# Two more units of the MLP's down projection done plainly, between the fast up units and the fast passes

## The chip, the cores and the metric

The kernel runs on one core of one Trainium2 chip. The metric is the device time of one execution in microseconds: the median of three runs is 1788.47 us (1786.55 to 1789.25).

## The reference

Two requests, a prompt of 256 tokens and a sample of 512, pass through the same two-layer encoder. All is float32. Cut to what matters here:

```
for layer in range(2):
    x = x + attention(rmsnorm(x)) @ w_out         # layer 0: neighbourhood and grouped-query heads
                                                  # layer 1: differential heads
    h = rmsnorm(x, ln_mlp[layer])                 # 768 tokens x 1024 features
    x = x + square(relu(h @ w_up)) @ w_down       # w_up 1024x4096, w_down 4096x1024
return rmsnorm(x, ln_f)
```

The change touches only the MLP line, in both layers.

## The kernel before

**Layout.** Features lie on the 128 partitions, the 768 tokens of both requests side by side along the row. `x` is eight tiles of 128x768. A float32 product is made of three float32r products: each operand is split into a high part (ScalarE copies it to float32r) and a low part (VectorE subtracts), and TensorE adds high x high, high x low and low x high. So each weight tile costs a copy (lines 90, 95) and a subtraction (line 91), or, for some quarters, a second ScalarE copy and an accumulating DMA issued by GpSimd (`wsplit_acc`, lines 95 to 97).

**Fast products.** Most of the MLP is done by Strassen's scheme in Winograd's form: a 2x2 block product takes seven products instead of eight. A *unit* is 256 of the 4096 hidden features. `up_fast` (line 948) makes one unit: seven products of 12 matmuls (`product`, line 940; line 945 is the matmul), 128x384 each, with results in the PSUM tiles upx, upy and upz. It then prepares seven *forms* of the unit's activations, the operands that the down projection's seven products will want, in one staging tile `hf` (two buffers), and SyncE stores them to DRAM (line 998, 1344 KB). `quarters` (line 905) loads the weights of one unit or pass as two tiles `wraw` (three buffers) and builds four tile pairs `whi`/`wlo` (four buffers) of sums and differences of the weight quarters, on VectorE (line 921) and ScalarE.

`down_fast` (line 1038) makes one *pass*: for a pair of output tiles p (0 to 3) it takes the units k0 to k1 of the table `PASSES` (14 entries), runs seven products of 3 matmuls for each unit (PSUM tiles dnx, dny, dnz), and adds each product to `x` (`onto`, line 1046: VectorE). `Forms.need` (line 1017) loads the forms back (line 1020) into `hf`, and splits them on ScalarE (line 1032) and VectorE (line 1033) into the tiles that the string `HOMES` names in order: `h` the four pairs hh/hl, `T` the six pairs Th/Tl, `x` the eight pairs xh/xl. T and x hold the input of the up units until the last of them.

**Plain products.** Per layer, four hidden tiles (half the size of a unit each) at the start are done plainly: `up_plain` and `down` (line 1080; matmul in `proj_feat`, line 222; results dna, dnb; additions in line 1090). The last two units ("rest") go up by the fast scheme without forms and down plainly, in layer 0 with `down` again, in layer 1 in `final` (line 1094). So a layer runs: plain group up and down, 12 fast units up, 2 rest units up, 14 passes, last plain group. `mlp` (line 1145) holds this order.

**What sets the order.** Each engine executes its own queue in order. The order in the queues is made by a scheduler from the program's order, priorities and buffers that come free; all waits are semaphores. SyncE's queue carries all weight loads, form loads and form stores; GpSimd's the accumulating DMAs.

## Time and profile before

| | |
|---|---|
| median of three runs | 1788.47 us (1786.55 to 1789.25) |
| profiled execution | 1786.56 us |
| its span, first to last instruction | 1784.8 us |
| TensorE busy (PE) | 1733.3 us, 11098 matmuls |
| VectorE busy (DVE) | 1267.9 us |
| ScalarE busy (ACT) | 946.9 us |
| mean granted TensorE clock | 0.991 |

The stages of the span that matter here, by the first and last matmul of each name:

| stage | layer 0, us | layer 1, us |
|---|---|---|
| plain group, down | 413.9 to 447.0 | 1312.1 to 1345.2 |
| 14 fast up units (12 with forms, 2 rest) | 446.9 to 650.8 | 1345.2 to 1549.2 |
| 14 fast passes | 650.8 to 843.8 | 1549.2 to 1740.5 |
| last plain group | 843 to 875.5 | 1738 to 1775 (with the final norm) |

How to read it: a matmul's recorded duration (334 ns for 128x384) overlaps with the next one's, so a busy share says little; what counts is how many matmuls a stretch of time holds.

### The profile page before, as it was taken

The page shows a single profiled execution, that of the slowest core. Times are in us where ns is not written, and L with a number is a line of the kernel's source. Part 1 is how long each engine was busy: PE and PEld are TensorE (multiplying, and loading weights), DVE is VectorE, ACT ScalarE, POOL GpSimd, SP SyncE. Part 2 cuts the span into 40 slices and gives each one's busy share as a digit, 9 for nine tenths or more (in the row PEclk, how much of TensorE's full clock was granted, in tenths as well). Part 3 has the DMA queues.
Part 4 walks back from the last instruction along what each step waited for, and adds up shares of the span by engine and source line. Part 5 has one row for each costly group of instructions (what it writes and reads, how often), then busy time and mean ns, then how long its engine had stood idle before and what let it go on. Part 6 is the DMA issues. An engine that isn't in the chain of part 4 may idle for free.

```text
span 1784.8 us, 28991 instructions
## 1 busy us (share of the span) xinstructions
PE 1733.3 (97%) x11098; PEld 1645.2 (92%) x11098; DVE 1267.9 (71%) x2458; ACT 946.9 (53%) x1981; POOL 248.4 (14%) x330
## 2 busy tenths in 40 slices
PE   7999999999999989999999999999999999989998
PEld 7878888899999989999999999988899999989997
DVE  7877646479566668886566767676696666688875
ACT  6765544344566665453435555554455666655534
POOL 3421000020000001111221312220200000011111
PEclk9999999999999999999999999999999999999999
DMA  5111222312565676764411101112124666777542
GB/s 166 48 34 40 65 86 90 124 34 66 143 188 183 213 251 177 234 172 99 153 48 48 48 25 46 54 57 95 36 66 132 184 186 186 244 216 230 157 102 83
DMA packets 61546, 214.49 MB, mean 120 GB/s; under 512 B 7136, under 2 KB 12512, under 8 KB 55264
## 3 DMA queue, kind: packets, MB, share of 16 engines
q1 hardware_dynamic: 47296, 190.08, 32.1%
q0 software_dynamic: 12096, 19.93, 7.1%
q10 hardware_dynamic: 2016, 2.64, 0.5%
q8 instruction: 87, 1.43, 0.3%
q14 instruction: 51, 0.42, 0.1%
HBM read 169.37 MB, written 42.47 MB: 119 GB/s over the span
## 4 chain that ended last, share of the span: by engine, by line
PE 84%; DVE 6%; DMA 4%; ACT 2%; issue 2%; POOL 1%; POOLq 0%; SPq 0%; DVEq 0%; ACTq 0%
PE upx L945 13%; PE dnx L945 9%; PE dqk L209 8%; PE upz L945 6%; PE dnz L945 4%; PE dvp L209 4%; PE upc L880 4%; PE opa L222 4%; PE upy L945 3%; PE dna L222 3%; PE dnb L222 3%; PE npa L222 2%; PE dny L945 2%; PE ds L288 2%; PE dpv L731 2%
## 5 line engine op out<-in xcount | busy, mean ns | idle before, releaser
L91 DVE TENSOR_TENSOR wlo<-wraw,whi 128x1024 fp32r<-128x1024 f32 (+3 forms) x232 | 224.3, 967 | 140.0 <-ACT whi L90 139.6
L90 ACT ACTIVATE whi<-wraw 128x1024 fp32r<-128x1024 f32 (+3 forms) x228 | 193.6, 849 | 177.8 <-PE dnx L945 70.5
L209 PE MATMUL dqk<-whi,xh 128*128 128x256 f32 x384 | 115.6, 301 | 0.0
L209 PE MATMUL dqk<-whi,xl 128*128 128x256 f32 x384 | 108.6, 283 | 0.0
L209 PE MATMUL dqk<-wlo,xh 128*128 128x256 f32 x384 | 108.4, 282 | 0.0
L716 ACT ACTIVATE de<-ds,m 128x512 f32<-128x512 f32 (+1 forms) x96 | 58.3, 612 | 79.7 <-DVE m L714 79.6
L97 POOL DMA_DIRECT2D wlo<-in_w_down_dram x56 | 49.3, 913 | 364.3 <-ACT wlo L96 277.3
L95 ACT ACTIVATE whi<-wraw 128x512 fp32r<-128x512 f32 (+3 forms) x84 | 49.2, 586 | 91.4 <-PE upy L945 36.6
L97 POOL DMA_DIRECT2D wlo<-in_w_up_dram x28 | 24.7, 883 | 452.6 <-DVE hf L963 301.1
L1046 DVE TENSOR_TENSOR x<-x,dnx 128x384 f32<-128x384 f32 x112 | 61.6, 550 | 33.9 <-PE dnx L945 33.1
L209 PEld LDWEIGHTS dqk<-whi,xh 128*128 128x128 f32 x384 | 73.1, 190 | 8.5 <-issue 7.7
L945 PE MATMUL upx<-Th,whi 128*128 128x384 f32 x224 | 74.9, 335 | 0.0
L945 PE MATMUL upx<-Th,wlo 128*128 128x384 f32 x224 | 74.8, 334 | 0.0
L945 PE MATMUL upx<-Tl,whi 128*128 128x384 f32 x224 | 74.8, 334 | 0.0
L945 PE MATMUL upx<-xh,whi 128*128 128x384 f32 x224 | 74.8, 334 | 0.0
L945 PE MATMUL upx<-xl,whi 128*128 128x384 f32 x224 | 74.8, 334 | 0.0
L945 PE MATMUL upx<-xh,wlo 128*128 128x384 f32 x224 | 74.8, 334 | 0.0
L90 ACT ACTIVATE whi<-ws 128x1024 fp32r<-128x1024 f32 (+3 forms) x56 | 56.0, 999 | 35.3 <-PE dnz L945 17.1
L209 PEld LDWEIGHTS dqk<-wlo,xh 128*128 128x128 f32 x384 | 73.3, 191 | 0.0
L209 PEld LDWEIGHTS dqk<-whi,xl 128*128 128x128 f32 x384 | 73.1, 190 | 0.0
L921 DVE TENSOR_TENSOR ws<-wraw 128x1024 f32<-128x1024 f32 (+3 forms) x56 | 64.1, 1145 | 11.3 <-DMA wraw<-in_w_down_dram 7.9
L158 POOL TENSOR_TENSOR acc<-acc,sq 128x384 f32<-128x384 f32 (+2 forms) x28 | 39.0, 1394 | 233.4 <-ACT sq L153 232.6
(350 smaller groups left out, 6103.0 us busy)
## 6 DMA issues: line engine op xcount, KB each, us to landing
wraw<-in_w_up_dram SPq DMA_DIRECT2D x64, 512.0 KB, 3.6
h<-hf SPq DMA_DIRECT2D x24, 1344.0 KB, 5.1
hf<-h SPq DMA_DIRECT2D x24, 1344.0 KB, 7.6
wraw<-in_w_down_dram SPq DMA_DIRECT2D x56, 512.0 KB, 3.8
wraw<-in_w_in_o_dram SPq DMA_DIRECT2D x24, 512.0 KB, 3.7
wlo<-in_w_down_dram POOLq DMA_DIRECT2D x40, 256.0 KB, 5.0
wraw<-in_w_in_e_dram SPq DMA_DIRECT2D x16, 512.0 KB, 3.7
wlo<-in_w_up_dram POOLq DMA_DIRECT2D x28, 256.0 KB, 6.0
```

Source lines behind the costliest of these rows:

```text
L90: nc.scalar.activation(hi, raw, AF.Copy)
L91: nc.vector.tensor_tensor(out=lo, in0=raw, in1=hi.bitcast(F32), op=ALU.subtract)
L95: nc.scalar.activation(hi, raw, AF.Copy)
L97: nc.gpsimd.dma_start(lo, src, accum_op=ALU.add)
L158: eng.tensor_tensor(out=self.acc[:, s], in0=self.acc[:, s], in1=sq, op=ALU.add)
L209: nc.tensor.matmul(ps[:, :256], st[:, tk], col(k, part, 0, 256), start=(k == 0 and i == 0), stop=(k == KD - 1 and i == 2))
L222: nc.tensor.matmul(ps[:, : e - s], lhs(k, part), mv[:, s:e], start=(k == 0 and i == 0), stop=(k == nk - 1 and i == 2))
L716: nc.scalar.activation(e, s, AF.Exp, bias=m, scale=1.0, accum_out=l2[:, c : c + 1])
L880: last = nc.tensor.matmul(ps, lhs(f0 + f, k, part), mv[:, s:e], start=(n == 0 and j == 0), stop=(n == KD - 1 and j == 2))
L921: add = lambda out, u, v: nc.vector.tensor_tensor(out=out, in0=u, in1=v, op=ALU.add)
L945: nc.tensor.matmul(ps, w[part][:, c], mv, start=(start and kk == 0 and j == 0), stop=(stop and kk == len(form) - 1 and j == 2), skip_group ...
L1046: nc.vector.tensor_tensor(out=xm[:, c], in0=xm[:, c], in1=ps, op=op)
```

## The change

1. The rest units keep their place at the end (now called "far"), but two more units are taken out of the fast passes. These "near" units go up by the fast scheme last, just before the passes. Their activations are not stored: `hparts` splits them at once from the staging tile into hh/hl, and a plain `down` of them runs between the up units and the first pass. Ten units with forms remain, and 12 passes.
2. `HOMES` starts with T and x (hh/hl are in use by the near group).
3. `keep_in_program_order` pins the first matmul of each product, and of each plain group's tile, so that TensorE's queue follows the program's order there.
4. Passes of two or three units use no accumulating DMA; their quarters are all split by ScalarE and VectorE.
5. ScalarE issues the stores of forms, and of the far units.
6. `wraw` has four buffers; the far units use the staging tile.

```diff
-NU = FF // P // 2 - GF
+NU = FF // P // 2 - 6
...
 PASSES = ((0, 0, 2), (1, 0, 3), (2, 0, 4), (3, 0, 4), (0, 2, 6), (1, 3, 7), (2, 4, 8), (3, 4, 8),
-          (0, 6, 10), (1, 7, 11), (2, 8, 12), (3, 8, 12), (0, 10, 12), (1, 11, 12))
+          (0, 6, 10), (1, 7, 10), (2, 8, 10), (3, 8, 10))
 
-HOMES = "hhh" + "TTTTTTxxxxxxxx" + "hhhh" + "TTTTTTxxxxxxxx" + "TTTTTTx"
+HOMES = "TTTTTTxxxxxxxx" + "hhhh" + "TTTTTTxxxxxxxx" + "TTT"
...
-        raw = rpool.tile([P, 1024], F32, tag="wraw", name="wraw", bufs=3)[:, :width]
+        raw = rpool.tile([P, 1024], F32, tag="wraw", name="wraw", bufs=4)[:, :width]
...
-                        nc.tensor.matmul(ps[:, : e - s], lhs(k, part), mv[:, s:e],
-                                         start=(k == 0 and i == 0), stop=(k == nk - 1 and i == 2))
+                        mm = nc.tensor.matmul(ps[:, : e - s], lhs(k, part), mv[:, s:e],
+                                              start=(k == 0 and i == 0), stop=(k == nk - 1 and i == 2))
+                        if pin and k == 0 and i == 0:
+                            tc.keep_in_program_order(mm)
...
+                if kk == 0 and j == 0:
+                    tc.keep_in_program_order(mm)
...
+        hs = [htiles(mp) for _ in range(2)] if kind == "near" else []
+
+        def done(i):
+            if hs:
+                hparts(*hs[i], st[:, 2 * i : 2 * i + 2])
...
-        if forms:
-            nc.sync.dma_start(kept, st)
-        else:
-            for i, t in enumerate(f):
-                nc.sync.dma_start(kept[:, 2 * i : 2 * i + 2].rearrange("p a b -> p (a b)"), t)
-        return kept
+        nc.scalar.dma_start(kept, st[:, :n])
+        return [kept]
+
+    def hparts(hi, lo, f):
+        f = f.rearrange("p a b -> p (a b)")
+        nc.scalar.activation(hi, f, AF.Copy)
+        nc.vector.tensor_tensor(out=lo, in0=f, in1=hi.bitcast(F32), op=ALU.subtract)
...
-        forms = Forms([up_fast(xs, T, mp) for _ in range(NU)], mp)
-        rest = [up_fast(xs, T, mp, False) for _ in range(GF // 2)]
+        units = lambda n, kind: [t for _ in range(n) for t in up_fast(xs, T, mp, kind)]
+        forms = Forms(units(NU, "forms"), mp)
+        rest = units(GF // 2, "far")
+
+        down(units(GF // 2, "near"), x, True)
         for p, k0, k1 in PASSES:
             forms.need(k1)
-            down_fast(x, p, forms.f[k0:k1], mp)
-            if (p, k1) == (3, NU):
+            down_fast(x, p, forms.f[k0:k1], mp, (11, 12) if k1 - k0 > 3 else ())
+            if (p, k1) == (1, NU):
                 hs = last_group(rest, mp)
...
-        nxt, nn = [], Norm(lambda: mp.tile([P, NT], F32, tag="sq", name="sq", bufs=1))
+        nxt, nn = [], Norm(lambda: staging(mp)[:, 0:2].rearrange("p a b -> p (a b)"))
```

The order of the weights in `w_down` follows the new table. In the changed file the lines behind the edits have moved: the matmuls of `product` are line 949, those of the plain groups line 223, the splits of forms lines 1049 and 1050, `hparts` lines 1018 and 1019.

TensorE's queue at the end of the up units of layer 0, before (upx is the last up product, dnx and dny the first fast pass):

```order
L945 MATMUL upx<-xl,whi 128x384
L945 MATMUL upx<-xh,wlo 128x384
L945 MATMUL dnx<-hh,whi 128x384
L945 MATMUL dnx<-hl,whi 128x384
L945 MATMUL dnx<-hh,wlo 128x384
L945 MATMUL dnx<-Th,whi 128x384
```

and now (dna and dnb are the near group's plain products):

```order
L949 MATMUL upx<-xl,whi 128x384
L949 MATMUL upx<-xh,wlo 128x384
L223 MATMUL dna<-hh,whi 128x384
L223 MATMUL dnb<-hh,whi 128x384
L223 MATMUL dna<-hl,whi 128x384
L223 MATMUL dnb<-hl,whi 128x384
```

192 matmuls of the near group now stand between the two phases.

ScalarE's queue from the end of the last near unit on, in the change (hf_7017 is that unit's staging tile, hh_7018 and hh_7020 its split halves, hf_7372 the first unit's forms on their way back, whi_7250 to whi_7312 plain weights, whi_7411 the first pass's weights):

```order
L90 ACTIVATE whi_7250<-wraw_7248 128x1024
L974 ACTIVATE hf_7017<-hf_7017 128x384
L1049 ACTIVATE Th_7382<-hf_7372 128x768
L1018 ACTIVATE hh_7018<-hf_7017 128x768
L973 ACTIVATE hf_7017<-upx_7013 128x384
L90 ACTIVATE whi_7312<-wraw_7310 128x1024
L974 ACTIVATE hf_7017<-hf_7017 128x384
L1049 ACTIVATE Th_7386<-hf_7372 128x384
L1018 ACTIVATE hh_7020<-hf_7017 128x768
L90 ACTIVATE whi_7411<-wraw_7406 128x256
```

The near unit's last half stands behind weight splits and form splits that the before had elsewhere in its queue.

ScalarE's queue at a unit's start in the up stage, before (hf_6343 is the new unit's staging tile, whi_6453 the next unit's weights):

```order
L964 ACTIVATE hf_6343<-upx_6339 128x384
L95 ACTIVATE whi_6453<-wraw_6448 128x512
L96 ACTIVATE wlo_6454<-wraw_6448 128x512
L90 ACTIVATE whi_6453<-wraw_6450 128x512
L967 ACTIVATE hf_6343<-hf_6343 128x384
```

and now:

```order
L970 ACTIVATE hf_6343<-upx_6339 128x384
L95 ACTIVATE whi_6453<-wraw_6448 128x512
L96 ACTIVATE wlo_6454<-wraw_6448 128x512
L1013 DMA h7_6310<-hf_6207 128x2688
L973 ACTIVATE hf_6343<-hf_6343 128x384
L970 ACTIVATE b12_6344<-upx_6339 128x384
```

The store of the unit before (hf_6207) now stands in ScalarE's queue, behind the copies that feed the accumulating DMA, and one weight split has moved further back.

More of the change, by code (lines that the diff above doesn't have):

```diff
@@ L944, in product, with up_fast @@
             for j, (part, mv) in enumerate(((0, fh), (0, fl), (1, fh))):
-                nc.tensor.matmul(ps, w[part][:, c], mv, start=(start and kk == 0 and j == 0),
-                                 stop=(stop and kk == len(form) - 1 and j == 2), skip_group_check=True)
-    def up_fast(xs, T, mp, forms=True):
+                mm = nc.tensor.matmul(ps, w[part][:, c], mv, start=(start and kk == 0 and j == 0),
+                                      stop=(stop and kk == len(form) - 1 and j == 2), skip_group_check=True)
+                if kk == 0 and j == 0:
+                    tc.keep_in_program_order(mm)
+    def up_fast(xs, T, mp, kind="forms"):
         ws = quarters("w_up", 512, mp, (11,))
@@ L955, in up_fast @@
         s5 = mp.tile([P, NH], F32, tag="st", name="s5", bufs=3)
+        st = staging(mp)
+        forms = kind == "forms"
         if forms:
-            st = staging(mp)
             b11, b21, t2, t1, t3, b22, t4 = (st[:, i] for i in range(7))
@@ L960, in up_fast @@
         else:
-            f = [mp.tile([P, NT], F32, tag=t, name="f", bufs=GF) for t in ("hh", "hl")]
-            b11, b12, b21, b22 = (t[:, c] for t in f for c in (ta, tb))
+            b11, b12, b21, b22 = (st[:, i] for i in range(4))
         op = lambda out, u, v, o: nc.vector.tensor_tensor(out=out, in0=u, in1=v, op=o)
@@ L987, in up_fast @@
         nc.vector.scalar_tensor_tensor(out=b12, in0=b12, scalar=0.0, in1=b12, op0=ALU.max, op1=ALU.mult)
+        done(0)
         if forms:
@@ L992, in up_fast @@
         relu2(b21, X, -1.0)
+        done(1)
         if forms:
             less(t4, t2, b21)
-        kept = dram.tile([P, 7 if forms else 4, NH], F32, name=f"h{len(store)}")
+        if hs:
+            return hs
+        n = 7 if forms else 4
+        kept = dram.tile([P, n, NH], F32, name=f"h{len(store)}")
         store.append(kept)
-        if forms:
-            nc.sync.dma_start(kept, st)
-        else:
-            for i, t in enumerate(f):
-                nc.sync.dma_start(kept[:, 2 * i : 2 * i + 2].rearrange("p a b -> p (a b)"), t)
-        return kept
+        nc.scalar.dma_start(kept, st[:, :n])
[4 more added lines that the diff above has]
+        nc.vector.tensor_tensor(out=lo, in0=f, in1=hi.bitcast(F32), op=ALU.subtract)
     store = []
@@ L1277, in _layout @@
     for w in wd:
-        parts.append(plain(w[:GF]))
+        parts += [plain(w[:GF]), plain(w[-GF:])]
         for ps in PASSES:
```

16 lines of the change are left out of this document (7 added, 9 removed).

## The prediction

> **What bounds the kernel now.** I first read the stretches of the two MLPs with their counts, then what TensorE waited for in them, then the chain of waits at the worst place. The windows are: layer 0's plain group, its up units, the head of its passes, the rest of the passes; then layer 1's head and rest. Columns: bounds and length in us, busy time and count by engine, granted clock, DMA share, GB/s.
>
> ```profile
> span 1784.8 us, 28991 instructions
> 413.87:447.00 33.13, 33.13 (x193) 33.13 (x193) 31.42 (x53) 13.55 (x26) 1.08 (x1) 1.00 0.22 59
> 446.88:650.70 203.82, 203.82 (x1178) 203.82 (x1177) 135.14 (x194) 127.01 (x229) 13.12 (x15) 1.00 0.61 186
> 650.70:708.90 58.20, 48.91 (x252) 46.51 (x251) 43.81 (x67) 29.88 (x48) 7.02 (x8) 0.91 0.78 226
> 708.90:840.40 131.50, 130.90 (x752) 129.61 (x750) 102.94 (x155) 62.56 (x94) 15.83 (x18) 1.00 0.59 162
> 1549.10:1591.00 41.90, 32.31 (x167) 29.97 (x166) 31.52 (x49) 21.67 (x36) 5.26 (x6) 0.96 0.80 242
> 1591.00:1737.40 146.40, 145.56 (x836) 144.32 (x834) 115.18 (x173) 70.78 (x105) 17.61 (x20) 1.00 0.60 166
> ```
>
> The 14 up units are 14 x 84 = 1176 matmuls (the window also counts one at each edge); 203.82 / 1176 = 0.1733 us each, with TensorE never idle. That is the pace of a 384-column matmul. The plain group keeps it as well: 192 x 0.1733 = 33.3 us, though VectorE is busy for 31.42 of them. The heads of the passes do not. Layer 0: 252 x 0.1733 = 43.7 us of work in 58.2, so 14.5 us lost. Layer 1: 167 x 0.1733 = 28.9 in 41.9, 13.0 lost. The rest of the passes loses 131.5 - 130.3 = 1.2 and 146.4 - 144.9 = 1.5. So **27.5 us are lost in the two heads and 2.7 behind them**, and elsewhere in the MLPs there is nothing to win but matmuls.
>
> What TensorE waited for, layer 0's passes and then layer 1's (us in total, times, longest), then the clock after the waits in layer 0, then pieces of the chain of waits there (start, length):
>
> ```profile
> PE dnx L945 <- DMA wlo<-in_w_down_dram: 6.0, 2, 3.0
> PE dnx L945 <- ACT whi L90: 2.0, 1, 2.0
> PE dnx L945 <- DVE x L1046: 1.7, 3, 0.7
> ...
> PE dnx L945 <- DMA wlo<-in_w_down_dram: 4.9, 2, 3.2
> PE dny L945 <- DMA wlo<-in_w_down_dram: 2.5, 1, 2.5
> PE dnx L945 <- ACT whi L90: 2.1, 1, 2.1
> ...
> 665.00:670.00 5.00, 3.77 (x14) 3.26 (x14) 1.67 (x4) 1.27 (x2) 0.00 (x0) 0.69 0.89 318
> 670.00:675.00 5.00, 3.64 (x11) 3.37 (x12) 4.79 (x7) 4.53 (x8) 0.87 (x1) 0.50 0.26 97
> ...
> 646.95 7.36 DMA wlo<-in_w_down_dram
> 657.70 7.80 DMA wlo<-in_w_down_dram
> ```
>
> The accumulating DMAs of the first two passes' weights take 7.4 and 7.8 us from issue to landing, in a stretch where the DMA engines are busy at 0.78 with form loads, weights and the last stores; the passes there are short (two and three units, 42 and 63 matmuls, 7.3 and 10.9 us), so nothing covers them. After 3 us of waiting the granted clock falls to 0.69 and 0.50 for a while: 14 and 11 matmuls in 5 us instead of 29. The lost 14.5 us are these waits plus the slow matmuls behind them.
>
> **The change, term by term.**
>
> *Matmuls.* Two units leave the passes: 2 x 7 products x 3 matmuls x 4 pairs = 168. The near group needs 4 tiles x 8 outputs x 2 halves x 3 = 192. Per layer 24 more, 24 x 0.1733 = 4.2 us; both layers **+8.3 us**, certain, since nothing else is on TensorE. The up stage keeps its 14 units.
>
> *The head's losses.* The first pass now starts 33.3 us after the last up product, behind the near group. In that time must be ready: the forms of units 0 and 1 for pass 0 and of 2 and 3 soon after, and the weights of passes 0 and 1. Durations and sizes:
>
> ```profile
> hf<-h SPq DMA_DIRECT2D x24, 1344.0 KB, 7.6
> h<-hf SPq DMA_DIRECT2D x24, 1344.0 KB, 5.1
> wlo<-in_w_down_dram POOLq DMA_DIRECT2D x40, 256.0 KB, 5.0
> L1090 DVE TENSOR_TENSOR x<-dna,x 128x384 f32<-128x384 f32 x8 | 4.5, 557 | 4.8 <-PE dna L222 4.6
> L91 DVE TENSOR_TENSOR wlo<-wraw,whi 128x1024 fp32r<-128x1024 f32 x18 | 22.0, 1220 | 2.8 <-ACT whi L90 2.8
> L91 DVE TENSOR_TENSOR wlo<-wraw,whi 128x512 fp32r<-128x512 f32 x12 | 8.2, 687 | 0.0
> L1046 DVE TENSOR_TENSOR x<-x,dnx 128x384 f32<-128x384 f32 x56 | 30.8, 550 | 16.6 <-PE dnx L945 16.2
> L1033 DVE TENSOR_TENSOR xl<-hf,xh 128x768 fp32r<-128x768 f32 x15 | 14.3, 953 | 1.1 <-ACT xh L1032 1.1
> L1032 ACT ACTIVATE xh<-hf 128x768 fp32r<-128x768 f32 x15 | 12.1, 835 | 4.8 <-PE dnx L945 2.2 <-PE dny L945 2.1 <-PE dnz L945 0.5
> L90 ACT ACTIVATE whi<-wraw 128x1024 fp32r<-128x1024 f32 x18 | 19.1, 1061 | 31.5 <-PE dnx L945 18.5 <-DVE wraw L921 4.7 <-PE dnb L222 3.8
> L96 ACT ACTIVATE wlo<-wraw 128x512 fp32r<-128x512 f32 x20 | 12.3, 615 | 0.0
> L968 ACT ACTIVATE f<-f 128x384 f32<-128x384 f32 x1 | 0.5, 523 | 0.0
> ```
>
> Bytes: four forms of 1344 KB are 5.5 MB and the two passes' weights (four tiles, 2 x 256 and 2 x 384 KB) 1.3 MB; at the head's 226 GB/s that is 30 us. The near group's own four weight tiles and the first form load go earlier, during the last up unit. So the bytes fit in 33.3 us, and form 3 is wanted only 18 us later. VectorE's queue between the last up product and pass 0 holds, by the program's order: 16 additions (8.9 us at 0.557), two plain weight subtractions (2.4), 13 full and 4 half form subtractions (12.4 + 2.2, the half ones taken as 0.55 like an addition of that width), the near unit's two (1.9), pass 0's weights and the start of pass 1's (5.3, by their widths from the rows of 512 and 1024 columns): 33.1 us. That is full, but what stands last in it belongs to later passes, and the first plain group ran without a wait at 31.42 of 33.13. Passes 0 and 1 have no accumulating DMA any more. I take the heads' losses as gone: **-27.5 us**. Bounds: half of them stay (-13.8), or the later waits go as well (-30.2).
>
> *New waits.* (a) The near group reads its fourth activation tile early: matmul 30 needs its high half 5.2 us after the last up product, matmul 32 its low half at 5.5. ScalarE gets there late: from the end of the fifth product (4.2 us before the end) its queue holds three weight copies of about 1.0 us, four full copies of forms and near halves at about 0.8, and six shorter ones at about 0.5, together some 9.2 us, so the high half comes at 5.1 and the low half, 0.95 us of VectorE later, at 6.1: a wait of 0.6 us if the first form lands in time for its split, which stands ahead in the same queue. Its load starts when the first near unit's staging tile comes free, about 11 us before the end, and takes 5.1 to 7.6 us; the split is due 5.8 us before the end. So 0.6 to 2.5 us; I take 1.2 per layer. (b) Pass 2 is the first with accumulating DMAs. Its weight slot comes free 3.1 us into pass 1; two copies of 0.6 us, the issue, and 5.0 us to landing (7.8 at worst above) end at about 10 to 12.5, wanted at 11.3 us: 0 to 1.2 us, I take 0.4. Waits of this size carry no loss of clock: in layer 1 a stretch with 2.2 us of idling kept the full clock:
>
> ```profile
> 1565.00:1570.00 5.00, 2.83 (x15) 2.08 (x13) 4.09 (x7) 1.96 (x4) 0.00 (x0) 1.00 0.61 252
> ```
>
> Together 1.6 per layer, **+3.2 us**, bounds 1.2 to 7.4.
>
> *The tail.* Passes 10 and 11 are now of two units: 7.3 us of TensorE against some 8.0 of VectorE each (7 additions of 0.55, seven weight operations of 0.4 to 0.7). Before, passes of two and one units stood there and the stretch lost almost nothing, with the scheduler weaving plain matmuls between them, which the pinned order forbids. Pass 9, of three units and 10.9 us, leaves VectorE some 3 us in hand. I take 0, at most 2 x 0.7 per layer, 2.8 in all.
>
> *Stores by ScalarE, four raw buffers, fewer form loads.* TensorE waits for nothing in the up stage, so freeing SyncE there earns nothing; four fewer form transfers per layer (two of them loads in the busy stretch) help the first term. The cost is below, as a rival.
>
> **Sum.** 1784.8 + 8.3 - 27.5 + 3.2 = 1768.8 us of span. The profiled execution took 1786.56, 1.8 more than its span, and the median of the runs is 1.9 above it: 1768.8 + 1.8 + 1.9 = 1772.5. I say **1772**.
>
> **Rivals.**
>
> *All hides.* New waits and the later waits vanish: 1772.5 - 3.2 - 2.7 = 1766.6. For it: the plain group before the up stage has no wait at all. Against: ScalarE's order at the near group.
>
> *Crowding.* ScalarE and VectorE, not DMA, become the bound: VectorE's 33 us in 33.3 slip, the first passes wait for their splits, and half of the heads' loss returns in place of the new waits: 1772.5 + 13.8 - 3.2 = 1783. For it: one form load waits for the split of another, in two staging tiles, and ScalarE waits in its queue for near matmuls before it may overwrite hh, with pass 1's weights behind. Against: those weights' slots come free only after pass 0's second product anyway.
>
> *The waits only move.* The same bytes and accumulating DMAs arrive as late after the near group as before it: all 27.5 return, at pass 2, which is the first with an accumulating DMA and by then needs four forms: 1772.5 + 27.5 - 3.2 = 1797, slower. It decides if the forms land more than some 15 us later than worked out. Against: in layer 0's later passes, of four units (14.6 us), the same mix runs at 0.59 DMA share and loses 1.2 us in 131.
>
> *Stores block ScalarE* (slower). A store waits on ScalarE for VectorE's last form operation; everything behind it waits too. In the up stage before, ScalarE and VectorE around the place where the store now stands:
>
> ```profile
> 597.31 0.61 ACT L96 ACTIVATE wlo<-wraw 128x512 fp32r<-128x512 f32 x1
> 599.32 0.47 ACT L964 ACTIVATE b<-upx 128x384 f32<-128x384 f32 x1
> 596.96 0.55 DVE L970 SCALAR_TENSOR_TENSOR hf<-hf 128x384 f32<-128x384 f32 x1
> 1774.96 0.34 ACTq L1127 DMA_DIRECT2D out_dram<-x  x1
> ```
>
> VectorE's last operation ends at 597.51, ScalarE's copy ahead of the store at 597.92: the store finds its data ready, with 0.4 us to spare, and costs about 0.34 us of issuing. The copy of upx at 599.32 must end before TensorE writes upx again, two products after the one that it copies, at about 600.9: 1.1 us of slack. Only if VectorE runs over 1.2 us late would TensorE wait; at 0.8 us for each of the 24 stores that is 19 us: 1772.5 + 19 = 1792. [...]
>
> **How the numbers follow.** Chances: forecast (1768 to 1777) 0.62, all hides 0.13, crowding 0.14, waits only move 0.05, stores block 0.04, no visible change for a cause not seen 0.02. The range reaches from just below "all hides" to almost "crowding": 1765 to 1782. A measurement of this kernel tells about 0.2% (3.6 us) from no change, so faster means below 1784.9: forecast, all hides and two thirds of crowding, 0.85; same 0.06; slower 0.09.
>
> **What would show it.** Right: the near group's 192 matmuls take 33.3 us plus one wait of about 1 us on the low half of hh; in the first 60 us of the passes some 340 matmuls, the clock at 1.00, no wait of 3 us on an accumulating DMA; up stage still 203.8 us. Wrong: TensorE waiting for wlo or form splits in passes 0 to 2 (crowding, or waits moved), idle time in the up stage (stores), or a first pass that starts late because form 0 or 1 landed after the near group.

## The result and the profile after

| | before | changed |
|---|---|---|
| median, us (range, runs) | 1788.06 (1786.55 to 1789.25, 4) | 1769.41 (1765.21 to 1770.32, 4) |
| profiled execution, span | 1786.56, 1784.8 | 1770.32, 1768.6 |
| ratio, 95% interval | | 0.9892 (0.9874 to 0.991) |

The change makes the kernel 1.1% faster. The forecast was 1772 (1765 to 1782), with a span of 1768.8.

The page of the changed kernel begins:

```profile
span 1768.6 us, 28926 instructions
PE 1731.0 (98%) x11146; PEld 1648.6 (93%) x11146; DVE 1253.4 (71%) x2446; ACT 924.8 (52%) x1933; POOL 223.8 (13%) x302
```

Then the stretches of the changed kernel, in the columns of the prediction's windows (bounds, length, PE, PEld, DVE, ACT and POOL busy with counts, granted clock, DMA share, GB/s): layer 0 from the first up product to the last plain one, its up stage, near group, head of the passes and the rest of them; then the same five for layer 1, to the last final product.

```profile
446.01:866.58 420.57, 417.31 (x2403) 416.06 (x2403) 300.42 (x443) 226.39 (x367) 31.32 (x31) 1.00 0.56 169
446.01:649.85 203.84, 203.84 (x1178) 203.84 (x1178) 129.80 (x183) 126.16 (x224) 11.36 (x13) 1.00 0.56 170
649.85:683.61 33.76, 33.56 (x193) 33.24 (x193) 28.22 (x45) 17.27 (x29) 0.00 (x0) 1.00 0.66 235
683.61:741.80 58.19, 57.10 (x329) 56.81 (x329) 49.34 (x76) 28.63 (x44) 7.01 (x8) 1.00 0.66 189
741.80:833.20 91.40, 89.42 (x515) 88.79 (x514) 70.43 (x111) 38.19 (x56) 5.29 (x6) 1.00 0.46 128
1337.56:1759.31 421.75, 419.18 (x2420) 414.01 (x2419) 296.99 (x446) 227.90 (x379) 30.11 (x32) 1.00 0.52 157
1337.56:1541.40 203.84, 203.84 (x1178) 203.84 (x1177) 130.17 (x183) 126.53 (x225) 11.44 (x13) 1.00 0.57 171
1541.40:1574.80 33.40, 33.40 (x194) 33.26 (x193) 28.42 (x45) 16.91 (x28) 0.00 (x0) 1.00 0.67 246
1574.80:1633.00 58.20, 56.67 (x325) 56.06 (x325) 48.06 (x75) 28.52 (x44) 7.03 (x8) 1.00 0.63 182
1633.00:1720.80 87.80, 86.75 (x500) 86.45 (x500) 68.38 (x108) 36.03 (x53) 5.28 (x6) 1.00 0.48 128
```

The same two whole stretches of the kernel before:

```profile
446.99:875.45 428.46, 418.57 (x2379) 414.88 (x2379) 307.84 (x449) 237.66 (x391) 43.78 (x45) 0.99 0.62 185
1345.20:1774.86 429.66, 419.01 (x2396) 411.10 (x2395) 304.39 (x452) 239.35 (x403) 42.40 (x46) 1.00 0.59 174
```

The MLPs became 428.46 - 420.57 = 7.9 and 429.66 - 421.75 = 7.9 us shorter, 15.8 of the span's 16.2. Each holds 24 matmuls more (2403 for 2379, 2420 for 2396). At 0.1733 us each, the head of layer 0's passes now loses 58.19 - 329 x 0.1733 = 1.2 us, where 14.5 were lost before; layer 1's loses 58.20 - 325 x 0.1733 = 1.9 instead of 13.0. Behind the heads 2.1 and 1.2 us are lost, 3.3 for the 2.7 of before. The clock stands at 1.00 throughout.

What TensorE still waits for in the changed kernel, from layer 0's near group to its last plain group, then the same in layer 1:

```profile
PE dnx L949 <- DVE x L1063: 3.1, 3, 1.3
PE dna L223 <- DVE hl L1019: 0.2, 1, 0.2
...
PE dnx L949 <- DVE x L1063: 2.6, 3, 1.0
```

No accumulating DMA and no form is waited for. The 0.2 us are the near group's wait for the low half of hh in layer 0. What is left is VectorE's additions of products to x (line 1063; line 1046 before), late by 0.6 to 1.3 us at three places per layer. The first of these, at pass 0, in VectorE's queue:

```profile
682.38 2.69 DVE L1050 TENSOR_TENSOR hl<-hf,hh 128x768 fp32r<-128x768 f32 x3
684.99 0.55 DVE L1105 TENSOR_TENSOR x<-dna,x 128x384 f32<-128x384 f32 x1
...
686.25 0.55 DVE L1063 TENSOR_TENSOR x<-x,dnx 128x384 f32<-128x384 f32 x1
```

Three splits of unit 4, which is not needed before the fifth pass, stand ahead of the near group's last additions and of pass 0's first. Pass 0 begins at 683.6, and its third product has to wait for that first addition until 686.8.

**How the experiments are read.** Runs differ by some microseconds for reasons outside the MLPs: the span less its two MLP stretches is 926.7 us in the kernel before and 926.3 in the changed one, and lies between 921.8 (no_acc) and 928.5 (no_pin_sp) in the others. A part of this shows in layer 1's plain up group, ahead of the up stage. The same first 48 matmuls went there at different granted clocks; in two kernels from below (no accumulating DMA in the down projection; none in the MLP at all):

```profile
1261.95:1270.81 8.86, 8.86 (x51) 8.56 (x51) 8.54 (x16) 4.86 (x10) 0.00 (x0) 1.00 0.00 0
1265.12:1277.61 12.49, 11.67 (x51) 11.35 (x51) 9.38 (x18) 5.07 (x10) 0.00 (x0) 0.73 0.14 42
```

That is 8.9 to 12.5 us for the same instructions; the kernel before took 9.0 there, at 1.00, and the changed one 11.3, at 0.85. So beside each median stand the lengths of the two MLP stretches in the profiled execution, which leave this out. They come from one execution of each kernel, and no run shows how much they vary between executions of the same kernel; a difference of a microsecond or two is to be read together with the waits in the traces.

| kernel | median, us | ratio to before (95%) | MLP layer 0, layer 1, us |
|---|---|---|---|
| before | 1786.6 to 1792.1 in five sets | 1 | 428.5, 429.7 |
| changed | 1769.41 | 0.9892 (0.9874, 0.991) | 420.6, 421.8 |
| near_behind_4 | 1794.75 | 1.0029 (1.0013, 1.0044) | 433.3, 434.1 |
| near_half | 1773.42 | 0.9907 (0.9887, 0.9927) | 423.2, 424.7 |
| acc_all | 1781.25 | 0.9956 (0.9941, 0.9972) | 426.4, 430.0 |
| before_no_short_acc | 1774.97 | 0.9926 (0.9899, 0.9953) | 419.7, 425.9 |
| before_T_homes | 1777.88 | 0.9952 (0.9931, 0.9972) | 423.2, 426.3 |
| before_no_acc | 1766.82 | 0.9885 (0.9871, 0.99) | 418.7, 419.5 |
| no_acc | 1763.26 | 0.988 (0.9855, 0.9904) | 418.3, 419.3 |
| no_acc_at_all | 1766.48 | 0.9887 (0.987, 0.9904) | 418.6, 421.3 |
| sp_raw3 | 1768.39 | 0.9909 (0.9887, 0.9931) | 419.7, 423.6 |
| no_pin | 1855.92 | 1.0391 (1.0367, 1.0414) | 460.2, 464.7 |
| no_pin_sp | 1766.59 | 0.9882 (0.9865, 0.9899) | 418.8, 419.8 |
| no_acc_sp | 1762.28 | 0.9841 (0.9815, 0.9867) | 416.6, 418.5 |

### The profile page after: what moved, and what is told of

Same layout as the page of the kernel before. It is cut to its first block, busy times and chain, and to the rows that moved or that the text cites. A ratio compares the mean times of both kernels' runs of the same rounds, so it can differ in the third digit from the quotient of the medians.

```text
span 1768.6 us, 28926 instructions
## 1 busy us (share of the span) xinstructions
PE 1731.0 (98%) x11146; PEld 1648.6 (93%) x11146; DVE 1253.4 (71%) x2446; ACT 924.8 (52%) x1933; POOL 223.8 (13%) x302
## 4 chain that ended last, share of the span: by engine, by line
PE 84%; DVE 7%; DMA 4%; ACT 2%; issue 2%; POOL 1%; POOLq 0%; DVEq 0%; ACTq 0%; SPq 0%
PE upx L949 12%; PE dnx L949 9%; PE dqk L209 8%; PE upz L949 6%; PE dnz L949 4%; PE dvp L209 4%; PE upc L883 4%; PE opa L223 4%; DMA hf<-h 3%; PE upy L949 3%; PE dnb L223 3%; PE dna L223 3%; PE npa L223 2%; PE ds L291 2%; PE dny L949 2%; PE dpv L734 2%
## 5 line engine op out<-in xcount | busy, mean ns | idle before, releaser
L91 DVE TENSOR_TENSOR wlo<-wraw,whi 128x1024 fp32r<-128x1024 f32 (+4 forms) x252 | 235.4, 938 | 144.1 <-ACT whi L90 143.7
L90 ACT ACTIVATE whi<-wraw 128x1024 fp32r<-128x1024 f32 (+4 forms) x248 | 203.4, 825 | 163.4 <-PE dnx L949 79.6
L95 ACT ACTIVATE whi<-wraw 128x512 fp32r<-128x512 f32 x56 | 35.2, 629 | 70.2 <-PE upy L949 36.6
L1063 DVE TENSOR_TENSOR x<-x,dnx 128x384 f32<-128x384 f32 x96 | 52.8, 550 | 22.8 <-PE dnx L949 22.7
L687 DVE SCALAR_TENSOR_TENSOR t<-dqk,rt,ropeO 128x128 f32<-128x128 f32 x192 | 57.6, 343 | 8.1 <-PE dqk L209 8.1
L158 POOL TENSOR_TENSOR acc<-acc,sq 128x384 f32<-128x384 f32 (+2 forms) x24 | 31.2, 1302 | 249.8 <-ACT sq L153 249.0
L90 ACT ACTIVATE whi<-ws 128x1024 fp32r<-128x1024 f32 (+2 forms) x52 | 51.8, 997 | 21.1 <-PE dnz L949 15.1
L97 POOL DMA_DIRECT2D wlo<-in_w_down_dram x28 | 24.6, 879 | 289.9 <-ACT wlo L96 148.4
```

The source lines that it names most:

```text
L90: nc.scalar.activation(hi, raw, AF.Copy)
L91: nc.vector.tensor_tensor(out=lo, in0=raw, in1=hi.bitcast(F32), op=ALU.subtract)
L97: nc.gpsimd.dma_start(lo, src, accum_op=ALU.add)
L687: nc.vector.scalar_tensor_tensor(out=tt[:, c].rearrange("p (a d) -> p a d", d=32), in0=ps[:, c].rearrange("p (a d) -> p a d", d=32), scalar=r,
L1063: nc.vector.tensor_tensor(out=xm[:, c], in0=xm[:, c], in1=ps, op=op)
```

## The experiments

### The place of the near group

near_behind_4, the changed kernel with:

```diff
-        down(units(GF // 2, "near"), x, True)
-        for p, k0, k1 in PASSES:
+        near = units(GF // 2, "near")
+        for i, (p, k0, k1) in enumerate(PASSES):
+            if i == 4:
+                down(near, x)
```

> The changed kernel with the near group's plain down projection (its 192 matmuls per layer, 33.3 us) moved behind the fourth pass; its units, their activation tiles and all other parts stay. TensorE does the same matmuls. Theory (the 33 us of plain matmuls between the last up product and the first pass are the cover under which the first forms and weights land): the first pass again starts right behind the up stage, with four forms to load, and most of the 27.5 us of the heads come back, since only the accumulating DMA of the first two passes is still gone: between 1783 and 1797 us. Rival (the gain comes from the two accumulating DMAs left out, the fewer forms and the stores by ScalarE, and the place of the group does not matter): 1769 to 1774.

Measured 1794.75 us, near the top of the theory's bounds and 0.3% slower than before. The heads of its passes, layer 0's and layer 1's, from its windows, and its longest wait in each:

```profile
646.86:707.73 60.87, 51.64 (x275) 49.02 (x274) 49.07 (x72) 29.17 (x43) 3.53 (x4) 0.94 0.66 211
1551.39:1611.61 60.22, 51.65 (x275) 49.03 (x275) 49.09 (x72) 29.21 (x43) 3.54 (x4) 0.94 0.67 214
...
PE dnx L949 <- ACT Th L1049: 6.4, 1, 6.4
...
PE dnx L949 <- ACT Th L1049: 6.3, 1, 6.3
```

60.87 - 275 x 0.1733 = 13.2 and 12.6 us are lost, nearly as much as in the kernel before, though the first two passes have no accumulating DMA. (The third and fourth, of four units, have; TensorE waits for one of theirs for 1.4 and 1.0 us.) The longest wait is for the second unit's form. The chain of waits there shows why it is late (start, length, what):

```profile
647.12 0.48 DVE Tl L1050
...
647.62 5.74 DMA hf<-h
...
653.38 0.03 ACT Th L1049
```

The load of the second form begins when VectorE has done the last split of the first. Of the two staging tiles, the near units, made last in the up stage, hold one until their own splits; the forms have the other. So it looks as if the near group needs to stand in front partly because of what its own units do to the staging tiles.

near_half, the same cut in two, with two of the group's four pairs of output tiles ahead of the passes:

```diff
-        down(units(GF // 2, "near"), x, True)
-        for p, k0, k1 in PASSES:
+        near = units(GF // 2, "near")
+        down(near, x, True, mqs=(0, 1))
+        for i, (p, k0, k1) in enumerate(PASSES):
+            if i == 4:
+                down(near, x, mqs=(2, 3))
```

> The changed kernel with half of the near group's output rows (96 matmuls, 16.7 us) ahead of the first pass and the other half behind the fourth. Theory (cover, counted in us: at about 226 GB/s the forms and weights of the first two passes are 30 us of transfers, but only those of the first pass, two forms and 0.5 MB of weights, 15 us, must have landed at its start): the first pass still finds its forms but the second and third run short, so about 5 to 12 us come back: 1774 to 1781. Rival (any cover of some 15 us is enough): 1769 to 1771. Second rival (the bytes of two passes must all have landed): half of the heads' losses return, 1783.

Measured 1773.42, between the first two answers: the medians differ by 4.0 us from the changed kernel, the MLPs by 2.7 and 2.9. The wait that comes back is on the accumulating DMA of the third pass, 1.5 us in layer 0 and 2.2 in layer 1; layer 0's:

```profile
PE dny L949 <- DMA wlo<-in_w_down_dram: 1.5, 1, 1.5
```

A wait of 1.0 us on a split stands behind the group's second half. Half of the cover would have done for the first forms; it is a late accumulating DMA that shows first.

### The accumulating DMAs of the short passes

Each half of the question alone: these DMAs back in the changed kernel (acc_all), and left out of the kernel before (before_no_short_acc).

```diff
-            down_fast(x, p, forms.f[k0:k1], mp, (11, 12) if k1 - k0 > 3 else ())
+            down_fast(x, p, forms.f[k0:k1], mp, (11, 12))
```

> The changed kernel with the accumulating DMA for rows 11 and 12 of the weights in every pass again, also in the six passes per layer of two and three units. Theory (the near group covers the first pass's, and the second pass's lands late because its slot comes free only in the first pass and a pass of two units is 7.3 us against 7.4 to 7.8 us from issue to landing): 2 to 5 us of waiting per layer, 1773 to 1779. Rival (with the cover in place these DMAs cost nothing): 1768 to 1771. Second rival (the copies that they save ScalarE and VectorE are worth more, since the waits left are on VectorE): 1764 to 1768.

Measured 1781.25, 11.8 us above the changed kernel and above the theory's 1779. The MLPs are 5.8 and 8.2 us longer. The theory's wait is there, 3.1 us in layer 0 (and 5.2 in layer 1), with the chain ahead of it:

```profile
PE dnx L949 <- DMA wlo<-in_w_down_dram: 3.1, 1, 3.1
...
688.02 7.30 DMA wlo<-in_w_down_dram
...
695.36 2.61 PE dnx L949 x7
697.97 2.24 PE dny L949 x7
```

The second pass's DMA takes 7.3 us from issue. The 14 matmuls behind the wait take 2.61 and 2.24 us, 0.35 each instead of 0.17: 2.4 us go to slow matmuls on top of the wait's 3.1. That was left out of the expectation. Another 1.3 us per layer go to a wait for the first of the two copies that feed such a DMA (line 95).

```diff
-        ws = quarters("w_down", len(fs) * P, mp, (11, 12))
+        ws = quarters("w_down", len(fs) * P, mp, (11, 12) if len(fs) > 3 else ())
```

> The kernel before with one edit: passes of two and three units (and of one) have no accumulating DMA, ScalarE and VectorE make those two rows' products instead. Theory (the waits of 6.0 and 7.4 us on these DMAs and the slow matmuls behind them are the greater part of the heads' 27.5 us, but with the waits gone the form loads and ScalarE's and VectorE's splits are the next to be late): a third to a half of the 27.5 us is won, 1774 to 1780. Rival (these DMAs are only the last of several things that come late together, behind the same busy DMA engines): 1784 to 1789. Second rival (they are the whole of it): 1761 to 1766.

Measured 1774.97, as the theory said: about 13.4 us of the kernel before's time is in these DMAs, against 18.7 won by the whole change. In the kernel before with and without them, and in the changed kernel with and without them, the medians are 1788.4, 1775.0, 1781.3 and 1769.4: the DMAs cost 13.4 and 11.8 us, the near group and all that goes with it win 7.1 and 5.6, after paying 8.3 for its matmuls.

before_T_homes is before_no_short_acc with the homes in the order of the change:

```diff
-HOMES = "hhh" + "TTTTTTxxxxxxxx" + "hhhh" + "TTTTTTxxxxxxxx" + "TTTTTTx"
+HOMES = "TTTTTTxxxxxxxx" + "hhhh" + "TTTTTTxxxxxxxx" + "TTTTTTxxxx"
```

> The kernel before without the accumulating DMA in its passes of two and three units (as in the run that took 1774.97 us), and with the forms' homes in the changed kernel's order: the first unit's forms go to the six T tiles, which the up products read to the end of the stage, instead of three h tiles that are free during it. No plain group in between. Theory (without a cover the first form can only be split once the last up product is through: the group behind the fourth pass lost 6.4 us per layer to that wait, and about as much to slow matmuls behind it): 10 to 14 us more than 1774.97, 1785 to 1789. Rival (what was lost there came from something else, such as weights ordered otherwise by the moved group): 1773 to 1778.

Measured 1777.88, the rival. TensorE waits for no form in its passes; the longest waits, 4.3 and 3.6 us, are on an accumulating DMA of a pass of four units. So the homes are not what made the form late in near_behind_4. The staging tile, which here serves the forms alone, remains as the likeliest cause, with the chain above for it; no run changed the staging by itself, so this is argued and not shown.

### All accumulating DMAs of the down projection

no_acc is the changed kernel with none of them, before_no_acc the kernel before with none:

```diff
-            down_fast(x, p, forms.f[k0:k1], mp, (11, 12) if k1 - k0 > 3 else ())
+            down_fast(x, p, forms.f[k0:k1], mp, ())
...
-        ws = quarters("w_down", len(fs) * P, mp, (11, 12))
+        ws = quarters("w_down", len(fs) * P, mp, ())
```

> The changed kernel without any accumulating DMA in the down projection, also not in the six passes per layer of four units. Theory (these DMAs land in time in passes of 14.6 us and save ScalarE a negation and VectorE two subtractions of 0.95 to 1.2 us per pass; VectorE's additions are what TensorE waits for now): no gain, 0 to 4 us more than the changed kernel, 1769 to 1773. Rival (an accumulating DMA costs wherever it stands, by its traffic in the DMA engines or by the copies that wait behind it): 2 to 5 us less, 1764 to 1767.

> The kernel before without any accumulating DMA in the down projection; no near group, 12 units in passes, stores by SyncE. Leaving these DMAs out of the passes of two and three units gave 1774.97 us; leaving them out altogether won 6 us more in the changed kernel. Theory (the two effects are separate: the near group still covers the first passes' forms and weights, worth some 5 us beyond its 8.3 us of matmuls): 1767 to 1772, 4 to 8 us slower than the changed kernel without these DMAs (1763.26). Rival (without these DMAs there is nothing left to cover, and the near group only costs its 8.3 us): 1755 to 1762. Second rival (in the kernel before VectorE and ScalarE have no room for the extra copies at the head of the passes): 1773 to 1778.

no_acc gave 1763.26, just below the rival's bounds: 2.2 and 2.4 us less in the MLPs, the rest outside them. Its MLP in layer 0 shows that the expectations had one thing wrong: such a DMA saves VectorE a subtraction, but costs ScalarE a second copy (VectorE 308.43 for 300.42 us, ScalarE 219.50 for 226.39):

```profile
443.10:861.43 418.33, 417.04 (x2403) 416.10 (x2403) 308.43 (x457) 219.50 (x353) 19.02 (x17) 1.00 0.51 162
```

before_no_acc gave 1766.82, at the edge of the theory's bounds and no slower than the changed kernel. Its median is 3.6 us above no_acc's, but its MLPs are only 0.4 and 0.2 us longer; the rest lies outside them. The MLPs of before_no_acc, each followed by the head of its passes, and its waits in layer 0:

```profile
444.78:863.49 418.71, 415.57 (x2379) 413.16 (x2379) 322.03 (x477) 224.37 (x363) 19.14 (x17) 1.00 0.55 175
648.62:706.70 58.08, 54.94 (x300) 52.95 (x300) 55.16 (x85) 30.27 (x46) 0.00 (x0) 0.97 0.61 218
1334.47:1753.96 419.49, 416.13 (x2396) 409.51 (x2395) 317.93 (x480) 226.08 (x374) 17.75 (x18) 1.00 0.51 163
1538.31:1580.20 41.89, 38.75 (x216) 36.85 (x216) 40.71 (x65) 22.02 (x35) 0.00 (x0) 1.00 0.65 232
...
PE dnx L945 <- DVE wlo L91: 1.6, 1, 1.6
PE dnx L945 <- ACT whi L90: 1.4, 1, 1.4
```

In the same lengths of time as in the prediction's heads (58.2 and 41.9 us) stand 300 and 216 matmuls instead of 252 and 167. The heads lose 58.08 - 300 x 0.1733 = 6.1 and 4.5 us, 10.6 instead of 27.5: **the accumulating DMAs were 16.9 us of the heads' losses, and only the rest is there for a cover**. Leaving them out of the short passes alone (before_no_short_acc) already does this for layer 0, with 300 matmuls in 58.12 us. VectorE now is the one that is full, 55.16 of 58.08 us. The MLPs of before_no_acc and no_acc, 418.7 and 419.5 against 418.3 and 419.3, are the same: with no such DMA the near group's 8.3 us of matmuls buy back just the 8.3 us that they cost. The expected 4 to 8 us in favour of the group came from taking its effect as independent of these DMAs in the longer passes; by the MLPs it is not.

no_acc_at_all leaves them out of the up stage as well:

```diff
-        ws = quarters("w_up", 512, mp, (11,))
+        ws = quarters("w_up", 512, mp, ())
```

> The changed kernel without any accumulating DMA in the down projection, and without the one per unit in the up stage. Theory (what these DMAs cost in the passes is that ScalarE makes two copies in a row and the weights land 5 us later; in the up stage TensorE waits for nothing, so nothing is won there, and VectorE's 9.7 us per unit of 14.6 have room for 0.7 more): as without them in the passes alone, 1761 to 1766. Rival (VectorE, which then does one more subtraction per unit, makes TensorE wait in the up stage): 5 to 15 us more, 1768 to 1778. Second rival (their traffic costs TensorE's clock or other transfers something everywhere): 1755 to 1760.

Measured 1766.48, half a microsecond above the theory's bound. The layer 0 stretch is as in no_acc (418.56 for 418.33 us), layer 1's 1.9 us longer, and its plain up group is the one of 12.49 us above. No gain in the up stage, and no loss that could be told: in the changed kernel, where such a DMA has 8.9 us (below), TensorE waits for none of them.

### The queues: stores, raw buffers, program order

sp_raw3:

```diff
-        raw = rpool.tile([P, 1024], F32, tag="wraw", name="wraw", bufs=4)[:, :width]
+        raw = rpool.tile([P, 1024], F32, tag="wraw", name="wraw", bufs=3)[:, :width]
...
-        nc.scalar.dma_start(kept, st[:, :n])
+        nc.sync.dma_start(kept, st[:, :n])
```

> The changed kernel with two of its small edits undone: the stores of the units go through SyncE's queue again, and three raw weight buffers instead of four. TensorE's order is the same. Theory (both were costed at nothing: TensorE waits for no weight in the up stage either way, and the stores' place in a queue is off the path): within 0.2% of the changed kernel, 1767 to 1772. Rival (SyncE's waits on the stores, 203 us of waiting in the kernel before, delay the loads of the near group and of the first forms and weights behind them): 3 to 8 us more, in the near group and the first two passes, 1772 to 1777.

Measured 1768.39: no difference that can be told from the changed kernel. The two edits together earn and cost nothing that the medians show; the MLPs are 0.9 us shorter and 1.8 longer, with single waits of 1.0 us on a weight copy in both layers and of 1.9 us on a form's split in layer 1. The two were not undone one at a time. The 203 us that the rival speaks of were misread: in the kernel before, SyncE's waits for its stores of forms (line 998) are 37.3 us in layer 0's up stage and 74.3 in all; the 203 us are waits of weight loads for a free buffer, in the changed kernel.

no_pin, without the pinned order (both places):

```diff
-                if kk == 0 and j == 0:
-                    tc.keep_in_program_order(mm)
...
-                        if pin and k == 0 and i == 0:
-                            tc.keep_in_program_order(mm)
```

> The changed kernel with TensorE's products not queued in program order but where the scheduler puts them. The prediction named only one place for it, the end of the passes, where the scheduler had woven plain matmuls between the short passes. Theory (the order hardly differs, and a wait of 1.0 us at the end of layer 0's passes is all that weaving could hide): within 0.2% of the changed kernel, 1767 to 1771. Rival (the pinned order is what keeps the near group ahead of the passes and the products in step, and without it products stand ahead of data that is not there): 3 us more or worse, over 1772.

Measured 1855.92, 87 us more than the changed kernel, 4% slower than before. What TensorE waited for in its two up stages:

```profile
PE upx L947 <- DMA wlo<-in_w_up_dram: 26.6, 9, 4.3
...
PE upx L947 <- DMA wlo<-in_w_up_dram: 29.1, 9, 4.6
```

One of these waits, in the timelines of GpSimd and TensorE and in windows over the wait, the time behind it and the time after that:

```profile
520.87 0.86 POOL L97 DMA_DIRECT2D wlo<-in_w_up_dram  x1 [19.91 <-DVE wlo L91]
...
525.22 0.34 PE L947 MATMUL upx<-xl,whi 128*128 128x384 f32 x1
528.00 0.69 PE L947 MATMUL upx<-xh,wlo 128*128 128x384 f32 x1 [2.44 <-DMA wlo<-in_w_up_dram]
...
531.57 0.33 PE L947 MATMUL upz<-xh,whi 128*128 128x384 f32 x1
533.68 0.33 PE L947 MATMUL upx<-xh,whi 128*128 128x384 f32 x1
...
525.00:528.00 3.00, 0.56 (x5) 0.24 (x3) 1.78 (x2) 1.84 (x3) 0.00 (x0) 1.00 1.07 388
528.00:531.40 3.40, 3.40 (x11) 3.40 (x12) 0.00 (x0) 0.00 (x0) 0.00 (x0) 0.50 0.73 251
531.40:536.00 4.60, 4.60 (x28) 4.60 (x27) 2.09 (x3) 2.19 (x4) 0.00 (x0) 1.00 0.02 7
```

The product at 525.04 is the next unit's first, whose weights' low part comes by an accumulating DMA issued at 520.87. The two products behind it (from 531.57 and 533.68) are the last two of the unit before: the scheduler has put the next unit's product ahead of them. It comes 4.2 us after the issue and waits till 528.0. In the changed kernel the same product comes last of the three, 8.9 us after the issue:

```profile
524.44 0.87 POOL L97 DMA_DIRECT2D wlo<-in_w_up_dram  x1 [13.69 <-DVE hf L969]
...
533.37 0.33 PE L949 MATMUL upx<-xh,whi 128*128 128x384 f32 x1
```

After the wait the clock stands at 0.50 for 3.4 us, 11 matmuls, and then at 1.00 again. Eighteen waits on this DMA, 0.9 to 4.6 us each and 55.7 us in all, and the slow matmuls behind some of them (granted clock 0.93 over either stage) make the up stages 246 and 249 us instead of 204.

no_pin_sp takes away the pin and the stores by ScalarE together (the two diffs of no_pin and the store's line of sp_raw3).

> The changed kernel without the pinned order and with the units' stores by SyncE again. Background: without the pin alone the time was 1855.92 us; TensorE then ran the next unit's first product ahead of the last two of the unit before, some 4 us earlier, and waited 18 times in the up stages, 55.7 us in all, for the accumulating DMA of that product's weights. In the program, this order comes up only where ScalarE issues the stores. Theory (the pin mends what the stores by ScalarE bring about in the scheduler's order, and neither earns anything by itself): within 0.2% of the changed kernel, 1766 to 1772. Rival (the pin is needed in any case, as four raw buffers and three groups of units let products be pulled ahead too): over 1800.

Measured 1766.59: the theory. Its up stages run without a wait, at 204 us. With sp_raw3 (pin kept, stores by SyncE, 1768.39) and no_pin (no pin, stores by ScalarE, 1855.92) this shows that the pin repairs what the stores by ScalarE do to the scheduler's order, and that the change would lose nothing with neither. In the passes the free order may even help a little: 418.8 and 419.8 us in the MLPs, 1.8 and 2.0 less than with the pin. TensorE's waits on VectorE in the passes are one per layer, 1.6 and 1.0 us, instead of three.

### A version that beats both

no_acc_sp joins no_pin_sp and no_acc.

> The changed kernel without accumulating DMAs in the down projection, with the stores by SyncE and without the pinned order: the two edits that won most in the MLPs, together. Counted from the start of the up stage to the last plain product of each MLP, the changed kernel took 420.6 and 421.8 us, the one without these DMAs 418.3 and 419.3, the one with stores by SyncE and no pin 418.8 and 419.8. Theory (both take away the same waits on VectorE, 1 to 1.7 us each, at the head and before the ninth pass, so they add up only in part): 417 to 418.5 and 418 to 419.5 in the MLPs, and 1760 to 1766 in all. Rival (they add up fully): 416.5 and 417.5, 1758 to 1762. Second rival (without the DMAs the unpinned order comes out worse): over 1767.

Measured 1762.28 (ratio to before 0.9841, 0.9815 to 0.9867, against runs of before at 1792.1), the lowest median of all, though by the medians it cannot be told from no_acc's 1763.26. Its two MLPs, and the passes of layer 0:

```profile
442.97:859.54 416.57, 416.57 (x2403) 416.08 (x2403) 307.74 (x457) 218.99 (x353) 18.99 (x17) 1.00 0.51 162
1330.43:1748.92 418.49, 418.49 (x2420) 414.07 (x2419) 304.05 (x460) 220.40 (x365) 17.75 (x18) 1.00 0.47 149
680.13:822.88 142.75, 142.75 (x824) 142.63 (x824) 124.36 (x195) 57.62 (x83) 0.00 (x0) 1.00 0.38 126
```

TensorE waits for nothing in either MLP: 824 matmuls in 142.75 us are 0.1732 each, the pace of the up stage. In layer 0 the two edits add up fully, as the rival said; in layer 1, 418.49 lies within the theory's bounds. With this plan of units and passes nothing is left to win in layer 0's MLP but matmuls.

## Why the prediction was right, and where it was not

**The sum.** Forecast for the MLPs: +8.3 - 27.5 + 3.2 = -16.0 us. Measured: -15.8. The span came out at 1768.6 for 1768.8. That the two agree so closely is in part luck, as the terms show.

**Matmuls, +8.3.** Right: 24 more in each MLP, at an unchanged pace.

**The heads' losses, -27.5.** Right in size: 3.1 of 27.5 us are left. The reason was given in one lump, bytes that fit under 33.3 us of cover and two passes without an accumulating DMA, and that was the weak step. The quoted waits of 6.0 and 7.4 us were on these DMAs, and should have been a term of their own: by before_no_acc, 16.9 of the 27.5 us go when the DMAs go, with no cover at all. The list of bytes was not the limit: with half the cover (near_half) no form is late at the first pass. For the other 10.6, what VectorE and ScalarE have to do in the heads is the likelier limit, since the waits left in before_no_acc are on them (1.6 and 1.4 us); no run takes that work away by itself. The prediction also let the clock fall after 3 us of waiting. In layer 0 of the kernel before that holds for one of two such waits: behind the one of 3.02 us that ended at 654.35 the clock stayed at 1.00 (655 to 660 us), behind the one of 3.00 us that ended at 665.55 it fell, to 0.69 and then 0.50 (665 to 675). That waits of some 2 us carry no loss of clock holds for the window quoted with it, and not for no_pin (0.50 behind 2.44 us).

**New waits, +3.2.** Right as a sum by accident. (a) The near group's low half of hh was to cost 1.2 us per layer: that wait is there in layer 0, but of 0.2 us, and the near groups lost 33.76 - 193 x 0.1733 = 0.3 us and nothing. That is less than the 0.6 us given for a first form that lands in time: the place of the wait was right and its size was not. (b) The third pass's accumulating DMA was to cost 0.4: no wait on it, though near_half shows that it is next in line (1.5 us). In their place came VectorE's additions in the passes, 3.1 and 2.6 us of waiting, among them the 3.1 us that the heads still lose; the kernel before had 1.7 and 0.8 us of such waits. It is the "crowding" rival on a small scale: its price was set at half of the heads' losses, 13.8 us, and its place at the weights' and forms' splits. Where the queue is shown above, it is the splits of a later unit, placed ahead of additions, and each wait stays near a microsecond.

**The tail, 0 (at most 2.8).** Part of the VectorE waits of layer 0 lies there: the one at 829.9 us is 0.7 long. Plain matmuls woven in hide it, as said of the kernel before: with a free order (no_pin_sp) it is gone.

**Stores, raw buffers, order: 0.** Right for the change as a whole (sp_raw3, no_pin_sp), but for a reason that the prediction did not see. It weighed the stores by ScalarE as a queue that blocks, 1792 us, and the pinned order as something that only forbids weaving. No run shows the 0.8 us per store from which the 1792 was added up: in the changed kernel the row of ScalarE behind a store waited for VectorE 0.15 us at 16 of the 24 stores and not at all at the others, and TensorE waited for nothing in either up stage. The danger lay between the two: the stores change the order in which the scheduler emits products, and that costs 87 us unless the order is pinned. A step that the prediction took as three separate edits was one edit with its repair.

**The rivals.** "The waits only move" did not happen; near_behind_4 is nearest to it, at 1794.75 for the forecast 1797, when the cover is taken away. "All hides" forecast 1766.6, and no_pin_sp, where the pinned order is gone, measured 1766.59; but one wait per layer stays there, so the mechanism is not quite that.

What stays open: why leaving the accumulating DMAs out of the four-unit passes shortens the waits for VectorE's additions (from 3.1 to 1.3 us in layer 0, from 2.6 to none in layer 1, where a wait of 0.6 us on ScalarE's copy of a weight stands instead). VectorE then does more (308.4 for 300.4 us in layer 0), in another order; the free order alone had nearly the same effect with the DMAs kept. That it is the order is argued from this, not shown by a run that changes the order alone.

## What to carry to other kernels

When TensorE waits for one kind of transfer at the head of a stage, price leaving that transfer out by itself before covering it with work: here a one-line edit to the kernel before (before_no_acc) gives what the whole change gives, and the cover only pays for its own matmuls. An accumulating DMA that saves VectorE a subtraction must have its whole way from issue to landing, 4.9 and 6.1 us by the medians of the changed kernel and up to 9.1 in the kernel before, before the product that needs it. And when an edit touches queues, ask what the scheduler will do with the order of the engine that bounds the time; a pin that seems idle may be holding up the stage.

## What the runs showed of the hardware

A wait of 2.44 us by TensorE (no_pin) was followed by 3.4 us at half the granted clock, 11 matmuls instead of 20, so a late transfer can cost more than its delay: 55.7 us of waiting made no_pin's two up stages, at a granted clock of 0.93 over each, 87.3 us longer. The length of the wait alone does not decide. One of 2.66 us in the same kernel (ended 1539.13) left the clock at 1.00, as did one of 3.02 us in the kernel before and those of up to 1.3 us in the changed kernel. In before_no_acc the clock stood at 0.70 from 665 to 670 us, behind two waits of only 1.6 and 1.4 us (ended 658.96 and 663.12). The window behind the wait of 2.66 us, and that stretch of before_no_acc:

```profile
1539.00:1542.40 3.40, 3.27 (x19) 3.27 (x20) 0.00 (x0) 0.82 (x2) 0.00 (x0) 1.00 0.79 281
...
665.00:670.00 5.00, 5.00 (x22) 5.00 (x22) 3.41 (x6) 2.98 (x5) 0.00 (x0) 0.70 0.64 210
```

What decides is not shown by these runs.

An accumulating DMA of 256 KB took 4.9 and 6.1 us, about twice as long as the 2.6 us of a plain load of the same bytes, or more, by the changed kernel's list of transfers (last column: median us from issue to landing):

```profile
wlo<-in_w_up_dram POOLq DMA_DIRECT2D x28, 256.0 KB, 6.1
wlo<-in_w_down_dram POOLq DMA_DIRECT2D x28, 256.0 KB, 4.9
...
wraw<-in_w_down_dram SPq DMA_DIRECT2D x12, 256.0 KB, 2.6
```

The same first 48 matmuls of a plain up group took 8.9 to 12.5 us in different kernels, at granted clocks from 0.73 to 1.00. That is up to 3.6 of the 6.7 us by which the time outside the MLPs differs between kernels here.
